# Moving a grouped-query attention into the middle of a differential attention, and turning its value product round

## The chip, the cores and the metric

The kernel runs on one core of a Trainium2 chip. The metric is the device time of one execution in microseconds (us); the time before is the median of three runs. A profile is one execution recorded by the hardware profiler. PE is TensorE's matmul unit and PEld its weight loads, DVE is VectorE, ACT is ScalarE, POOL is GpSimd, SP is the engine that issues most of the transfers.

## The reference, cut to what matters

One transformer layer is computed for 512 latent tokens and 128 context tokens of width 1024, all in fp32. A token mixer with three groups of heads reads one modulated input; its outputs are concatenated and projected, and a squared-ReLU MLP follows.

```python
# group A: 4 heads, two softmax maps per head, values 128 wide
s = einsum('bqhmd,bkhmd->bhmqk', qb, k) * HEAD_DIM ** -0.5
p = softmax(s); w = p[:, :, 0] - lam * p[:, :, 1]
oa = einsum('bhqk,bkhe->bqhe', w, v)            # then RMS norm per head and token
# group B: a gated linear recurrence (scan) over chunks of 64 tokens
# group C: 4 query heads on 2 key/value heads, 64 wide
s = einsum('bqngd,bknd->bngqk', qb, k) * HEAD_DIM ** -0.5
oc = einsum('bngqk,bknd->bqngd', softmax(s), v)
mixed = concatenate([oa, ob, oc], -1) @ w_out
x = layernorm(ALPHA * x + g1 * mixed); hid = square(relu(mod(x) @ w_ff1))
y = layernorm(ALPHA * x + g2 * (hid @ w_ff2))
```

A latent token attends to 512 latent keys and 256 cached context keys, 768 in all. Context tokens attend to the 128 context keys alone.

## The kernel before

The 640 tokens are five tiles of 128 (`NT`): tile 0 is the context, tiles 1 to 4 are latent. Projections take the modulated input `xh`, `xl` (a value split by `split`, L89, into a high and a low part) against weights split in the same way, as three matmuls for each of eight blocks of the width (`mm3`, L126). Ahead of attention stand group B's scans and the projections of A's head 0; behind it stand the output projection (tiles `pswo`), the two MLP products (`psf`, `psy`) and the norms.

In the attention part a "unit" is one head of A and one latent tile t (`a_unit`, L805; 16 units, named A01 to A34 by head and t), or one query head j of C and one tile (`c_unit`, L932; 16 units, named C10 to C43 by t and j). Each unit has three steps:

- s1: the score product into a PSUM tile `pss` of 768 columns, the row maximum `nm` on DVE, and the exponential with its sum on ACT (`softmax_map`, L700). A unit of A has two maps, which DVE joins into one (L814). A unit of C has one, and DVE multiplies it by the reciprocal of its sum (L939).
- transposition of the 128x768 map in six pieces by PE (tiles `pst`, L720), copied to SBUF half by ACT and half by DVE (tiles `pT`).
- s3: the product with the values (`psav`). For A (`av`, L728) the transposed map is the stationary operand, the tokens come out on the partitions, and DVE scales the result (L821). ACT then squares it, and after a head's last tile `a_norm` (L764) normalizes the head, transposes it back (tiles `psao`) and writes `mixed`. For C (L952) the values, 64 wide, are the stationary operand and the transposed map moves through. Two query heads with the same values go to the two halves of the partitions, so that C's output stands already transposed; ACT copies it to `mixed` (L954).

`pipeline` (L828) emits step n's s1, then the transposition of unit n-1, then s3 of unit n-2, and whatever a table (`put`, from L1100 on) hangs behind step n: tiles of the next head's projection, its preparation (`prep`: transposing queries and keys and splitting them, L657 and L671; `prep_ctx`: the head's context tokens), pieces of the modulation (`ada`) and the rest of group B. The framework's scheduler then fixes one order of instructions on each engine; an engine works through its own order and waits wherever it must. PSUM has two buffers for each of three kinds of tile (`ps_mm`, `ps_o`, `ps_s`, L284 to L290); `pss` takes `ps_s`, the projections and C's transposed queries and keys take `ps_mm`.

The order of heads is A0, A1, A2, A3, C. Projections of the next head stand among the units of the one before; C, the last, has none to stand among its own. Once `mixed` is complete for a block of the width, `split` makes the output projection's input from it, for tokens 0 to 383 and then for 384 to 639.

Of the kernel before, what the change touches and what calls it, by code (L numbers as in the profile page):

```python
# [19 lines left out]
P = 128  # L20
# [43 lines left out]
def hybrid_layer_kernel(ctx: ExitStack, tc: tile.TileContext, T):  # L64
# [563 lines left out]
    def new_grp(name, par, ck, cv):  # L628
        g = Grp()
        g.name = name  # L630
        g.par = par
        g.qtags = ("a_q0", "a_q1", "b_b1", "b_k1") if name == "C" else ("a_q0", "a_q1", "b_k0", "b_k1")
        g.ltags = ("a_kl", "u6", "u3", "b_b0")
        g.src = (ck, cv)
        g.z = []
        return g
# [98 lines left out]
    def a_gemm(h):  # L735
        g = new_grp(f"A{h}", h % 2, T["cache_a_k"][:, h * P : (h + 1) * P], T["cache_a_v"][:, h * P : (h + 1) * P])
# [68 lines left out]
    def a_unit(g, h, t):  # L805
# [12 lines left out]
        def s3(pT):  # L818
# [4 lines left out]
            if t == NT - 1:  # L823
                a_norm(g, h)
# [20 lines left out]
    def c_gemm():  # L845
        g = new_grp("C", 0, T["cache_c_k"], T["cache_c_v"])
# [39 lines left out]
    def c_ctx(g):  # L886
# [8 lines left out]
        pr = p1t("b_xs", [P, 512], name="cpC")  # L895
# [32 lines left out]
    def c_prep(g):  # L928
        queries(g, [(0, ((0, 0), (1, 0)))])
# [167 lines left out]
    def put(n, *fs):  # L1097
        post.setdefault(n, []).extend(fs)
# [310 lines left out]
```

## Time and profile before

| | |
|---|---|
| median of three runs | 951.87 us (950.09 to 952.92) |
| the profiled execution, its time and its span | 952.96 us, 951.2 us |
| PE busy | 912.9 us (96% of the span), 6133 instructions |
| DVE busy | 573.6 us (60%), 1123 instructions |
| ACT busy | 432.7 us (45%), 916 instructions |
| PE's share of the chain that ended last | 80%; DVE 11%, ACT 3%, DMA 3% |
| mean granted clock of TensorE | 0.986 |

PE is busy nearly throughout, so the stages that matter are those in which it is not, or in which its clock is low. Of the 40 slices on the page the one from 357 to 381 us is marked 8 for PE and 8 for the clock; it lies between A's last projections and C's units. A busy PE is a pipelined one: the record of a matmul includes its passage through the array, so short waits of PE are hidden in its busy time, and what a matmul costs in a row of them is the distance between starts.

### The profile page before, as it was taken

Reading aid. Unit: us, or ns where it says so; the run is one execution under the profiler, and the core shown is the slowest. Engines: PE = TensorE matmul, PEld = TensorE weight load, DVE = VectorE, ACT = ScalarE, POOL = GpSimd, SP = SyncE. Lnnn points to the kernel's source line nnn. Section 1 sums busy time; section 2 is a strip of 40 time slices with the busy share of each in tenths; the row PEclk is TensorE's granted clock in tenths of the full one; section 3 lists DMA queues with packets and bytes.
Section 4 is the critical chain, followed back from the end, with each engine's and each line's share of the span. In section 5 each row is a group of like instructions: output and inputs, shape, how many; then the busy total and the mean of one; then the engine's idle time right before and its main releaser. Section 6 shows DMA issues by size and latency. Waiting matters only on the chain.

```text
span 951.2 us, 15540 instructions
## 1 busy us (share of the span) xinstructions
PE 912.9 (96%) x6133; PEld 792.2 (83%) x6133; DVE 573.6 (60%) x1123; ACT 432.7 (45%) x916; POOL 53.5 (6%) x108
## 2 busy tenths in 40 slices
PE   6989898999999998999999999999999999999996
PEld 4778886889889786678899999999998888888884
DVE  2378998988876888873794313243236343563448
ACT  3566675466664657651583212222225333243320
POOL 2200010210100000001000000000000000000000
PEclk9998999999999998999999999999999999999998
DMA  9951525433021320113223234342122222142102
GB/s 260 290 157 54 157 86 162 108 92 94 19 78 39 117 65 13 68 45 133 89 68 111 61 95 133 121 125 73 61 90 84 72 68 88 34 152 80 67 23 88
DMA packets 95752, 90.82 MB, mean 95 GB/s; under 512 B 5792, under 2 KB 81280, under 8 KB 95680
## 3 DMA queue, kind: packets, MB, share of 16 engines
q1 hardware_dynamic: 91936, 82.50, 28.9%
q0 software_dynamic: 3552, 7.27, 2.5%
q8 instruction: 48, 0.79, 0.3%
q14 instruction: 24, 0.20, 0.1%
q10 hardware_dynamic: 192, 0.08, 0.0%
HBM read 86.41 MB, written 3.41 MB: 94 GB/s over the span
## 4 chain that ended last, share of the span: by engine, by line
PE 80%; DVE 11%; ACT 3%; DMA 3%; issue 1%; SPq 1%; DVEq 0%; ACTq 0%
PE psf L1271 8%; PE psy L130 8%; PE psf L1272 8%; PE psf L1273 8%; PE psy L129 8%; PE psy L128 8%; PE psA L129 2%; PE psA L130 2%; PE psavA L730 2%; PE psA L128 2%; PE pswo L130 2%; PE pswo L129 2%; PE pswo L128 2%; DVE b_st L560 2%; PE psavC L952 2%
## 5 line engine op out<-in xcount | busy, mean ns | idle before, releaser
L1271 PE MATMUL psf<-xh,wf_h 128*128 128x320 f32 x512 | 158.7, 310 | 0.0
L1272 PE MATMUL psf<-xl,wf_h 128*128 128x320 f32 x512 | 158.1, 309 | 0.0
L1273 PE MATMUL psf<-xh,wf_l 128*128 128x320 f32 x512 | 158.1, 309 | 0.0
L130 PE MATMUL psy<-wg_h,xl 128*128 128x512 f32 x320 | 127.7, 399 | 0.0
L129 PE MATMUL psy<-wg_l,xh 128*128 128x512 f32 x320 | 126.1, 394 | 0.0
L128 PE MATMUL psy<-wg_h,xh 128*128 128x512 f32 x320 | 125.5, 392 | 0.0
L91 DVE TENSOR_TENSOR xl<-hid,xh 128x640 fp32r<-128x640 f32 x64 | 52.1, 824 | 86.5 <-ACT xh L90 86.5
L90 ACT CAST xh<-hid 128x640 fp32r<-128x640 f32 x64 | 45.6, 727 | 121.7 <-PE psy L129 116.2
L1271 PEld LDWEIGHTS psf<-xh,wf_h 128*128 128x128 f32 x512 | 96.3, 188 | 1.7 <-issue 1.2
L1272 PEld LDWEIGHTS psf<-xl,wf_h 128*128 128x128 f32 x512 | 96.3, 188 | 0.0
L1273 PEld LDWEIGHTS psf<-xh,wf_l 128*128 128x128 f32 x512 | 96.3, 188 | 0.0
L1276 DVE TENSOR_TENSOR hid<-hid,psf 128x320 f32<-128x320 f32 x64 | 31.1, 486 | 106.5 <-ACT hid L1275 106.4
L1275 ACT ACTIVATE hid<-psf 128x320 f32<-128x320 f32 x64 | 28.0, 438 | 119.9 <-PE psf L1273 119.9
L129 PEld LDWEIGHTS psy<-wg_l,xh 128*128 128x128 f32 x320 | 60.1, 188 | 15.6
L128 PEld LDWEIGHTS psy<-wg_h,xh 128*128 128x128 f32 x320 | 60.1, 188 | 14.3
L130 PEld LDWEIGHTS psy<-wg_h,xl 128*128 128x128 f32 x320 | 60.1, 188 | 13.7
L91 DVE TENSOR_TENSOR wf_l<-wf_r,wf_h 128x1024 fp32r<-128x1024 f32 x32 | 39.2, 1224 | 37.5 <-ACT wf_h L90 37.5
L128 PE MATMUL psA<-wa_h,xh 128*128 128x384 f32 x160 | 55.2, 346 | 0.0
L130 PE MATMUL psA<-wa_h,xl 128*128 128x384 f32 x160 | 54.9, 344 | 0.0
L129 PE MATMUL psA<-wa_l,xh 128*128 128x384 f32 x160 | 54.7, 343 | 0.0
L90 ACT CAST wf_h<-wf_r 128x1024 fp32r<-128x1024 f32 x32 | 33.7, 1054 | 32.8 <-PE psf L1272 28.4
L91 DVE TENSOR_TENSOR wg_l<-wg_r,wg_h 128x1024 fp32r<-128x1024 f32 x32 | 39.2, 1224 | 7.1 <-ACT wg_h L90 4.5
(475 smaller groups left out, 1897.2 us busy)
## 6 DMA issues: line engine op xcount, KB each, us to landing
wad<-in_w_ada SPq DMA_DIRECT2D x32, 512.0 KB, 4.8
wf_r<-in_w_ff SPq DMA_DIRECT2D x32, 512.0 KB, 3.9
wg_r<-in_w_ff SPq DMA_DIRECT2D x32, 512.0 KB, 3.6
adaw<-in_w_ada SPq DMA_DIRECT2D x32, 256.0 KB, 5.4
wa_r<-in_w_in SPq DMA_DIRECT2D x48, 128.0 KB, 2.9
wo_r<-in_w_out SPq DMA_DIRECT2D x8, 512.0 KB, 3.7
x<-in_x_sample SPq DMA_DIRECT2D x8, 256.0 KB, 4.9
wc_r<-in_w_in SPq DMA_DIRECT2D x4, 512.0 KB, 3.7
```

Of the source, the lines that this page charges most:

```text
L90: A.copy(hi, src)
L91: V.tensor_tensor(lo, src, f32(hi), op=ALU.subtract)
L128: PE.matmul(ps, s[0], m[0], start=start, stop=False)
L129: PE.matmul(ps, s[0], m[1], start=False, stop=False)
L130: PE.matmul(ps, s[1], m[0], start=False, stop=stop)
L560: V.scalar_tensor_tensor(dst, st[r, c, :], dec[r, c : c + 1], u(r, c), op0=ALU.mult, op1=ALU.add)
L730: PE.matmul(po, pT[:, c, :], vals(g, c, c0, n), start=(c == 0), stop=(c == NKC - 1))
L1271: PE.matmul(ps[:, 0:HALF], h, xh[:, k, sl], start=(k == 0), stop=False)
L1272: PE.matmul(ps[:, 0:HALF], h, xl[:, k, sl], start=False, stop=False)
L1273: PE.matmul(ps[:, 0:HALF], l, xh[:, k, sl], start=False, stop=(k == NK - 1))
L1275: A.activation(hs, ps[:, 0:HALF], AF.Relu)
L1276: V.tensor_tensor(hs, hs, ps[:, 0:HALF], op=ALU.mult)
```

## The change

C moves from behind A3 to between A0 and A1, and its sixteen units are ordered by value head n first and tile t second. The table of what stands behind which unit is new: C's projection stands among A0's units, A1's among C's, A2's behind C's last units and among A1's, A3's among A2's, and A3 comes last. C's buffers change with its neighbours. In `c_unit` the map is no longer scaled. The transposed map becomes the stationary operand, as in A; the values, 64 wide, move; DVE scales the 128x64 output by the reciprocal (in place of L939); and when a value head is complete, four transpositions and one copy put it into `mixed`. For the last head `a_norm` runs twice, for tiles 0 to 2 and for tiles 3 and 4.

```diff
-        g.qtags = ("a_q0", "a_q1", "b_b1", "b_k1") if name == "C" else ("a_q0", "a_q1", "b_k0", "b_k1")
-        g.ltags = ("a_kl", "u6", "u3", "b_b0")
+        qt, lt = ("a_q0", "a_q1", "b_k0", "b_k1"), ("a_kl", "u6", "u3", "b_b0")
+        g.qtags, g.ltags = (qt[2:] + qt[:2], lt[2:] + lt[:2]) if name == "C" else (qt, lt)
...
-        tags = ("u4", "u5", "a_vh", "a_vl") if name[0] == "C" else ("u4", "u5")
-        pT = p1t(tags[next(pt_count) % len(tags)], [P, NKC, P], name=f"pT{name}")
+        pT = p1t(("u4", "u5")[next(pt_count) % 2], [P, NKC, P], name=f"pT{name}")
...
-    def a_norm(g, h):
-        A.activation(g.ss, g.ss, AF.Ln, scale=1.0 / P, bias=epsA)
-        A.activation(g.ss, g.ss, AF.Exp, scale=-0.5)
-        for lo, hi in ((0, 1), (1, NT)):
+    def a_norm(g, h, *spans):
+        ss = g.ss[:, spans[0][0] : spans[-1][1]]
+        A.activation(ss, ss, AF.Ln, scale=1.0 / P, bias=epsA)
+        A.activation(ss, ss, AF.Exp, scale=-0.5)
+        for lo, hi in spans:
...
-            if t == NT - 1:
-                a_norm(g, h)
+            if h < NHA - 1:
+                if t == NT - 1:
+                    a_norm(g, h, (0, 1), (1, NT))
+            elif t in (2, NT - 1):
+                a_norm(g, h, (0, 3) if t == 2 else (3, NT))
...
     def c_unit(g, t, j):
         nm = f"C{t}{j}"
+        n = j // 2
 
         def s1():
-            sm = p1t("c_sm", [P, 1], bufs=3, name=f"sm{nm}")
-            pr = softmax_map(g, j, t, sm, 0, nm)
-            V.reciprocal(sm, sm)
-            V.tensor_scalar(pr, pr, sm, None, op0=ALU.mult)
+            rs = p1t("a_rs", [P, 3], bufs=4, name=f"rs{nm}")
+            pr = softmax_map(g, j, t, rs, 0, nm)
+            V.reciprocal(rs[:, 1:2], rs[:, 0:1])
+            g.rs[t, j] = rs
             return pr
 
         def s3(pT):
-            if j % 2 == 0:
-                g.pT = pT
-                return
-            if j == 1:
-                g.po = ps_mm(f"psavC{t}")
-            n = j // 2
-            for c in range(NKC):
-                v = vals(g, c, n * HD, HD)
-                for r, w in ((slice(0, HD), g.pT), (slice(HD, P), pT)):
-                    PE.matmul(g.po[r, n * P : (n + 1) * P], v, w[:, c, :], start=(c == 0), stop=(c == NKC - 1))
-            if j == 3:
-                A.copy(mixed[:, 6:8, t * P : (t + 1) * P], g.po[:, 0:256].rearrange("p (i n) -> p i n", i=2))
+            if t == 1 and j % 2 == 0:
+                g.o = p1t(("ao2", "ao")[n], [P, NLAT // P, P], name=f"co{n}")
+            po = ps_o(f"psav{nm}")
+            av(po[:, 0:HD], g, pT, n * HD, HD)
+            V.tensor_scalar(g.o[:, t - 1, j % 2 * HD : (j % 2 + 1) * HD], po[:, 0:HD], g.rs[t, j][:, 1:2], None, op0=ALU.mult)
+            if t == NT - 1 and j % 2:
+                pt = ps_o(f"psco{n}")
+                for i in range(NLAT // P):
+                    PE.transpose(pt[:, i * P : (i + 1) * P], g.o[:, i, :], ident)
+                A.copy(mixed[:, 6 + n, P:NTOK], pt)
...
+    order = [("a", 0, t, 0) for t in range(1, NT)]
+    order += [("c", NHA, t, 2 * n + j) for n in range(2) for t in range(1, NT) for j in range(2)]
+    order += [("a", h, t, 0) for h in range(1, NHA) for t in range(1, NT)]
...
-    put(13, lambda: tiles(4, 0))
+    put(3, lambda: prep_ctx(4))
+    put(26, lambda: tiles(3, 3, 4))
```

**C's preparation, PE.** From here on a row is one instruction of an engine's order: line, operation, output tile<-operands, shape. Names carry a running number. Before, from the last of C's transposed queries (`psqC0`) and keys (`pskC0`) on, through the transposition of the cached keys (`pskC512`):

```order
L678 MATMUL psqC0_4336<-ident_62,zC4_4279 128x128
L665 MATMUL pskC0_4355<-ident_62,zC4_4279 128x128
L720 MATMUL pstA330_4395<-ident_62,pA330_4297 128x128 x3
L720 MATMUL pstA331_4400<-ident_62,pA330_4297 128x128 x3
L730 MATMUL psavA32_4405<-zA31_3649,pTA32_4312 128x128
L730 MATMUL psavA32_4405<-zA32_3739,pTA32_4312 128x128
L730 MATMUL psavA32_4405<-zA33_3769,pTA32_4312 128x128
L730 MATMUL psavA32_4405<-zA34_3843,pTA32_4312 128x128
L730 MATMUL psavA32_4405<-ckvA3_3848,pTA32_4312 128x128 x2
L705 MATMUL pssC10_4416<-k0C_4353,qC0_4341 128x512
L706 MATMUL pssC10_4416<-k0C_4353,qlC0_4342 128x512
L665 MATMUL pskC512_4364<-ident_62,ckvC_4333 128x128 x2
```

After, from the same two instructions on, through C's context scores (`psccs`) to the first projection matmul of A1:

```order
L678 MATMUL psqC0_3029<-ident_62,zC4_2984 128x128
L665 MATMUL pskC0_3048<-ident_62,zC4_2984 128x128
L665 MATMUL pskC512_3057<-ident_62,ckvC_3026 128x128 x2
L922 MATMUL pscC_3110<-ident_62,zC0_2718 128x128 x3
L894 MATMUL psccs_3119<-cqkC_3108 128x128 x2
L894 MATMUL psccs_3119<-cqkC_3108,cqC_3109 128x128 x2
L128 MATMUL psA10_3146<-wa1_h0_2996,xh_69 128x384
```

Before, the transpositions of unit A33, the product of A32 and C10's first scores stood between C's last transposed tile and `pskC512`. Now `pskC512`, C's transposed context (`pscC`) and its scores follow directly, and A1's projection comes behind them.

**C's preparation, ACT.** After, the row of ACT from the first copy of C's transposed queries to the copies of its transposed context, which `psccs` reads (four more copies like the last one follow):

```order
L686 ACTIVATE qC0_3034<-psqC0_3029 64x512
L668 CAST k0C_3046<-pskC0_3048 64x512
L710 ACTIVATE pA040_3072,smA04_3064<-pssA040_3065,nmA040_3070 128x768
L710 ACTIVATE pA041_3081,smA04_3064<-pssA041_3074,nmA041_3079 128x768
L688 ACTIVATE qC0_3034<-psqC0_3029 64x512
L686 ACTIVATE qC1_3040<-psqC0_3029 64x512
L668 CAST k1C_3047<-pskC0_3048 64x512
L761 ACTIVATE sqA02_3106,ass0_2586<-ao0_2585 128x128
L90 CAST wa2_h0_3702<-wa2_r0_3700 128x768
L688 ACTIVATE qC1_3040<-psqC0_3029 64x512
L668 CAST k0C_3046<-pskC512_3057 64x256
L923 COPY cqkC_3108<-pscC_3110 128x128
```

Before, the unit of A among these copies was A33 and C's first exponentials; now it is A04, with a weight split for A2 (`wa2_h0`).

**The end of the attention part, PE.** Before, from C's last transposition to the first matmul of the output projection:

```order
L720 MATMUL pstC431_5009<-ident_62,pC43_4975 128x128 x3
L952 MATMUL psavC4_4990<-pTC43_5003,zC1_4156 64x128
L952 MATMUL psavC4_4990<-pTC42_4979,zC2_4197 64x128
```

(eight more of L952 follow, two for each block of keys, and then)

```order
L952 MATMUL psavC4_4990<-pTC43_5003,ckvC_4333 64x128
L1181 MATMUL psabg100_5088<-grows_64,sel_63 128x512
L1181 MATMUL psabg101_5092<-grows_64,sel_63 128x512
L128 MATMUL pswo00_5119<-wo0_h0_5097,xh_69 128x512
```

After, from the last head's first norm (`psao30`) on:

```order
L771 MATMUL psao30_5004<-ident_62,ao3_4699 128x128
L719 MATMUL pstA340_5013<-ident_62,pA340_4966 128x128
L771 MATMUL psao30_5004<-ident_62,ao3_4699 128x128
L719 MATMUL pstA340_5013<-ident_62,pA340_4966 128x128
L719 MATMUL pstA341_5018<-ident_62,pA340_4966 128x128 x3
L729 MATMUL psavA33_5023<-zA31_4522,pTA33_4981 128x128
```

(the rest of that product and the six matmuls of unit A34's follow, and then)

```order
L729 MATMUL psavA34_5033<-ckvA3_4661,pTA34_5012 128x128 x2
L771 MATMUL psao33_5045<-ident_62,ao3_4699 128x128 x2
L1179 MATMUL psabg100_5112<-grows_64,sel_63 128x512
L1179 MATMUL psabg101_5116<-grows_64,sel_63 128x512
L128 MATMUL pswo00_5143<-wo0_h0_5121,xh_69 128x512
```

The output projection stood behind a unit of C; now it stands behind A3's last unit and behind the transposition of its norm (`psao33`).

**The end of the attention part, DVE.** After, a piece of DVE's row ahead of the output projection:

```order
L708 TENSOR_REDUCE nmA331_4929<-pssA331_4924 128x1
L91 TENSOR_TENSOR wo1_l0_5302<-wo1_r0_5301,wo1_h0_5303 128x1024
L722 COPY pTA32_4937<-pstA321_4943 128x384
L708 TENSOR_REDUCE nmA340_4964<-pssA340_4959 128x1
L812 RECIPROCAL rsA33_4933<-smA33_4914 128x2
L821 TENSOR_SCALAR ao3_4699<-psavA31_4948,rsA31_4791,lam_647 128x128
L813 SCALAR_TENSOR_TENSOR rsA33_4933<-smA33_4914,lam_647,rsA33_4933 128x1
L708 TENSOR_REDUCE nmA341_4973<-pssA341_4968 128x1
L814 SCALAR_TENSOR_TENSOR pA330_4922<-pA331_4931,rsA33_4933,pA330_4922 128x768
L91 TENSOR_TENSOR xl_70<-mixed_83,xh_69 128x384
L91 TENSOR_TENSOR xl_70<-mixed_83,xh_69 128x256
L722 COPY pTA33_4981<-pstA331_4987 128x384
```

Before, these steps of A3 stood among the evacuations of C's projection, and C's units followed. Now the row holds the last units of A and splits for the output projection (`wo`, `xl`), with no projection of another head beside it.

## Rows read from the trace of the kernel before

**Rows 1.** The page, busy us, share of the span and instructions of engines.
```profile
PE 912.9 (96%) x6133; PEld 792.2 (83%) x6133; DVE 573.6 (60%) x1123; ACT 432.7 (45%) x916; POOL 53.5 (6%) x108
```
**Rows 2.** Windows: length; busy of PE, PEld, DVE, ACT, POOL; clock, DMA share, GB/s.
```profile
199.00:353.00 154.00, 152.48 (x950) 134.45 (x950) 124.97 (x251) 93.52 (x235) 13.25 (x22) 1.00 0.24 73
359.00:384.00 25.00, 20.41 (x125) 16.27 (x124) 21.59 (x42) 18.66 (x53) 0.52 (x1) 0.86 0.06 22
384.00:426.00 42.00, 40.56 (x349) 29.39 (x348) 33.24 (x64) 24.96 (x54) 3.22 (x6) 1.00 0.14 45
```
**Rows 3.** Timeline, C's preparation: start, length, engine, instruction, [idle <-releaser].
```profile
360.03 0.33 PE L678 MATMUL psqC<-ident,zC 128*128 128x128 f32 x1 [1.00 <-DVE zC L623]
...
365.31 0.59 ACT L688 ACTIVATE qC<-psqC 64x512 fp32r<-64x512 f32 x1
...
365.90 0.38 PE L665 MATMUL pskC<-ident,ckvC 128*128 128x128 f32 x2
```
**Rows 4.** Timeline, PE's value products, A's then C's, and maps of C.
```profile
252.27 1.16 PE L730 MATMUL psavA<-zA,pTA 128*128 128x128 f32 x8
253.26 0.61 PE L730 MATMUL psavA<-ckvA,pTA 128*128 128x128 f32 x4
253.63 0.36 PE L706 MATMUL pssA<-k0A,qlA 128*128 128x256 f32 x1
...
397.80 0.98 PE L952 MATMUL psavC<-pTC,zC 128*64 128x128 f32 x13 [0.29 <-ACT pTC L725]
...
399.25 0.50 PE L705 MATMUL pssC<-k0C,qC 128*128 128x512 f32 x1
...
400.85 0.84 PE L720 MATMUL pstC<-ident,pC 128*128 128x128 f32 x6
```
**Rows 5.** Timeline, weight loads ahead of matmuls with 2 and 64 columns.
```profile
186.95 0.52 PEld L976 LDWEIGHTS psada<-selc,ada 128*128 128x128 f32 x4
187.49 0.75 PEld L553 LDWEIGHTS psu<-mixed,b_kht 64*128 64x128 f32 x12
```
**Rows 6.** Groups of ACT, 199:426: count | busy us, mean ns | idle before.
```profile
L710 ACT ACTIVATE pA<-pssA,nmA 128x768 f32<-128x768 f32 x32 | 28.8, 902 | 3.3 <-DVE nmA L708 2.9 <-PE pstA L720 0.3
L90 ACT CAST wa_h<-wa_r 128x768 fp32r<-128x768 f32 x9 | 7.5, 830 | 3.8 <-PE psA L130 3.6 <-DMA wa_r<-in_w_in 0.2
L686 ACT ACTIVATE qA<-psqA 64x512 fp32r<-64x512 f32 x7 | 4.1, 590 | 0.6 <-PE psqA L678 0.4
L923 ACT ACTIVATE cqkC<-pscC 64x128 f32<-64x128 f32 x1 | 0.3, 274 | 0.0
```
**Rows 7.** Groups of DVE, 199:426, same columns.
```profile
L708 DVE TENSOR_REDUCE nmA<-pssA 128x1 f32<-128x768 f32 x32 | 30.2, 952 | 2.3 <-PE pssA L706 1.9
L814 DVE SCALAR_TENSOR_TENSOR pA<-pA,rsA,pA 128x768 f32<-128x768 f32 x16 | 16.2, 1013 | 0.2
L939 DVE TENSOR_SCALAR pC<-pC,smC 128x768 f32<-128x768 f32 x16 | 9.8, 613 | 0.0
L723 DVE COPY pTA<-pstA 128x384 f32<-128x384 f32 x16 | 8.8, 552 | 2.5 <-PE pstA L720 2.5
L821 DVE TENSOR_SCALAR ao<-psavA,rsA,lam 128x128 f32<-128x128 f32 x16 | 6.5, 407 | 5.5 <-PE psavA L730 5.5
L91 DVE TENSOR_TENSOR wo_l<-wo_r,wo_h 128x1024 fp32r<-128x1024 f32 x5 | 6.0, 1207 | 0.0
L687 DVE SCALAR_TENSOR_TENSOR qlA<-psqA,qA 64x512 fp32r<-64x512 f32 x7 | 4.8, 687 | 0.7 <-ACT qA L686 0.5
L91 DVE TENSOR_TENSOR xl<-mixed,xh 128x256 fp32r<-128x256 f32 x6 | 2.5, 416 | 0.3 <-ACT xh L90 0.3
```
**Rows 8.** Timeline of DVE, first and last of 24 instructions nearly without a gap.
```profile
349.65 0.55 DVE L868 TENSOR_TENSOR zn<-psC,css 128x384 f32<-128x384 f32 x1
...
361.10 0.68 DVE L687 SCALAR_TENSOR_TENSOR qlC<-psqC,qC 64x512 fp32r<-64x512 f32 x1 [0.19 <-ACT qC L686]
```
**Rows 9.** Timeline of PE: the first matmul of the output projection.
```profile
426.15 0.40 PE L128 MATMUL pswo<-wo_h,xh 128*128 128x512 f32 x1
```

More of the change, by code (lines that the diff above doesn't have):

```diff
@@ L845, in c_gemm @@
     def c_gemm():
-        g = new_grp("C", 0, T["cache_c_k"], T["cache_c_v"])
+        g = new_grp("C", 1, T["cache_c_k"], T["cache_c_v"])
         g.kcol = 256
@@ L928, in c_prep @@
     def c_prep(g):
+        g.rs = {}
         queries(g, [(0, ((0, 0), (1, 0)))])
@@ L1089, in hybrid_layer_kernel, with make @@
     prep_ctx(0)
-    nu = NT - 1
-    units = [None] * (NHA * nu + 4 * nu)
+    order = [("a", 0, t, 0) for t in range(1, NT)]
+    order += [("c", NHA, t, 2 * n + j) for n in range(2) for t in range(1, NT) for j in range(2)]
+    order += [("a", h, t, 0) for h in range(1, NHA) for t in range(1, NT)]
+    units = [None] * len(order)
     pre, post = {}, {}
-    for h in range(NHA):
-        for t in range(1, NT):
-            n = h * nu + t - 1
-            pre.setdefault(n, []).append(lambda n=n, h=h, t=t: units.__setitem__(n, a_unit(gr[h], h, t)))
+    def make(n, kind, h, t, j):
+        units[n] = a_unit(gr[h], h, t) if kind == "a" else c_unit(gr[h], t, j)
+    for n, u in enumerate(order):
+        pre.setdefault(n, []).append(lambda n=n, u=u: make(n, *u))
     def put(n, *fs):
@@ L1100, in hybrid_layer_kernel @@
     put(0, lambda: b_out(3, parts[3]))
-    put(0, lambda: start(1))
-    put(0, lambda: tiles(1, 0))
-    put(1, lambda: tiles(1, 1))
-    put(1, lambda: tiles(1, 2))
-    put(1, lambda: tiles(1, 3))
-    put(1, lambda: tiles(1, 4))
-    put(2, lambda: b_final())
-    put(2, lambda: start(2))
-    put(2, lambda: prep(1))
-    put(2, lambda: prep_ctx(1))
-    put(3, lambda: tiles(2, 0))
-    put(4, lambda: tiles(2, 1))
-    put(6, lambda: tiles(2, 2))
-    put(6, lambda: tiles(2, 3))
-    put(6, lambda: tiles(2, 4))
@@ L1116, in hybrid_layer_kernel @@
-    put(6, lambda: prep(2))
-    put(6, lambda: prep_ctx(2))
-    put(7, lambda: ada(1, "b_b1"))
-    put(8, lambda: start(3))
-    put(8, lambda: tiles(3, 0))
-    put(8, lambda: tiles(3, 1))
-    put(9, lambda: tiles(3, 2))
-    put(9, lambda: tiles(3, 3))
-    put(10, lambda: tiles(3, 4))
-    put(10, lambda: prep(3))
-    put(10, lambda: prep_ctx(3))
-    put(13, lambda: start(4))
-    put(13, lambda: tiles(4, 0))
-    put(13, lambda: tiles(4, 1))
-    put(13, lambda: tiles(4, 2))
-    put(13, lambda: tiles(4, 3))
@@ L1132, in hybrid_layer_kernel @@
-    put(13, lambda: tiles(4, 4))
-    put(14, lambda: prep(4))
-    put(16, lambda: queries(gr[NHA], [(P, ((2, 1), (3, 1)))]))
-    put(18, lambda: prep_ctx(4))
-    put(19, lambda: ada(11, "b_k0"))
-    put(20, lambda: ada(8, "b_k0"))
-    for t in range(1, NT):
-        for j in range(4):
-            n = NHA * nu + (t - 1) * 4 + j
-            pre.setdefault(n, []).append(lambda n=n, t=t, j=j: units.__setitem__(n, c_unit(gr[NHA], t, j)))
+    put(0, lambda: start(4))
+    put(0, lambda: tiles(4, 0, 1))
@@ new lines, in hybrid_layer_kernel @@
+    put(1, lambda: tiles(4, 2, 3))
+    put(2, lambda: b_final())
+    put(2, lambda: tiles(4, 4))
+    put(2, lambda: start(1))
+    put(2, lambda: prep(4))
+    put(3, lambda: prep_ctx(4))
+    put(3, lambda: tiles(1, 0))
+    put(6, lambda: tiles(1, 1))
+    put(9, lambda: tiles(1, 2))
+    put(9, lambda: queries(gr[NHA], [(P, ((2, 1), (3, 1)))]))
+    put(11, lambda: tiles(1, 3))
+    put(13, lambda: tiles(1, 4))
+    put(15, lambda: start(2))
+    put(16, lambda: prep(1))
+    put(17, lambda: prep_ctx(1))
@@ L1142, in hybrid_layer_kernel @@
+    put(18, lambda: tiles(2, 0))
+    put(19, lambda: ada(1, "b_b1"))
+    put(21, lambda: tiles(2, 1, 2))
+    put(22, lambda: tiles(2, 3, 4))
+    put(22, lambda: start(3))
+    put(22, lambda: prep(2))
+    put(23, lambda: prep_ctx(2))
+    put(24, lambda: tiles(3, 0))
+    put(25, lambda: tiles(3, 1, 2))
+    put(26, lambda: tiles(3, 3, 4))
+    put(26, lambda: prep(3))
+    put(27, lambda: prep_ctx(3))
+    put(28, lambda: ada(11, "b_b1"))
+    put(29, lambda: ada(8, "b_b1"))
     pipeline(units, pre, post)
```

4 lines of the change are left out of this document (2 added, 2 removed).

## The prediction

> **What bounds the kernel now.** I read the page's engine line first: PE is busy 96% of the span [rows 1], so the reader should look for the places where it is not, or is slow. The windows by stage give them. From 199 to 353 us (A's heads with their projections) PE is busy 152.48 of 154 us at full clock; there is nothing to win there by order. From 359 to 384 it is busy 20.41 of 25 at a mean granted clock of 0.86, and from 384 to 426 it is busy 40.56 of 42 [rows 2]. That is the stretch of C, which has no next head's projection to fill with. Visible idle is 4.6 + 1.4 = 6.0 us, and 25 x 0.14 = 3.5 us are lost to the clock: 9.5 us at least.
>
> Some waits hide inside PE's busy time, so I price the work instead. In a dense piece two maps of scores take 399.25 to 400.85, 0.80 each, and six transpositions 0.84 with the passage through the array, some 0.70 without [rows 4]. A product of A takes 252.27 to 253.63 for 12 matmuls, 1.36 us or 113 ns each. C's product shows 22 records from 397.80 to 399.25, 66 ns each; for the twelve that one unit needs, 0.80 us [rows 4]. The 16 units of C are 16 x (0.80 + 0.70 + 0.80) = 36.8 us. What else PE does after 359 (three products of A, two transpositions, some 20 single transpositions, the modulation's pieces, the context's small products) comes to about 14 us by the same distances. The output projection begins at 426.15 [rows 9], 67.2 us after 359: 67.2 - 50.8 = 16 us are lost around C.
>
> **The change, part by part.**
>
> *C's lost time goes, at its old place: -16 us* (bounds -9.5, the visible part alone, and -18, if the distances above hold waits too). Its new place has A1's projection. But of 16 units only some have a projection tile behind them, and a map, an exponential and a copy still follow one another; for those without I keep 1.5 us, a tenth.
>
> *C's product, turned round.* The moving side shrinks to 64 columns, and 128x128 maps become the stationary side. No row shows this shape. Next to it lie A's product, the same load with 128 columns (113 ns), and four loads of 128x128 whose matmuls move 2 columns, in 0.52 us, at most 130 ns each [rows 5]. If 2 columns cost about as much as 128, it is the load that sets the distance, and 64 will too: 1.36 us for a unit, 0.56 more than before, times 16 = **+9.0 us**. The other row in the neighbourhood is that of twelve loads of 64 rows in 0.75 us, 63 ns [rows 5]; they are half as tall and lie in two halves of the array, as C's old operands did with their 64 columns, so I hold it to be the farther one. By it the term is 0. If the old product really ran at 60 ns, 24 in 1.45 us, the term is 16 x 0.64 = 10. Bounds 0 and +10. The Trainium skill, "TensorEngine Tiling (Array Packing)", section "When to Use Tiling", speaks against this edit: for a right side of at most 64 columns it advises swapping the operands and tiling the columns, for up to twice the rate, which is what the kernel before does. By that the new product would cost twice the old, 16 x 0.80 = 12.8 us more instead of 9; the two rows agree in direction, with 113 against 66.
>
> *Transpositions of C's output*: eight at 0.11 (the 0.70 above over six) = **+0.9 us** on PE.
>
> *The map's scaling on DVE*, 16 x 613 ns = 9.8 us [rows 7], goes; 16 scalings of 128x64 come, each at most the 407 ns of 128x128 [rows 7], 6.5 us. DVE has idle time among C's units (33.24 busy of 42 [rows 2]), so I take nothing for it; if DVE were the bound there, it would be a gain of 3.3 us. The two copies that take the place of four ACT copies, the buffers' new names and `a_norm` in two pieces issue no DMA; SP's and POOL's orders hold the same transfers with C's and A1's weights exchanged, at a DMA share of 0.24 [rows 2], at nothing. If a weight came late there, the price would be a matmul's wait, at most the 3.6 us by which ACT waited for PE in its weight casts over 227 us [rows 6].
>
> *C's preparation at its new place: +10 us* (6 to 14). PE's order is now: C's last transposed queries and keys, the cached keys (`pskC512`), the context (`pscC`), its scores (`psccs`), and only then A1's first projection. An engine waits in its order, so a wait ahead of `psccs` holds the filler back too. The first wait is for `zC4`. Before, PE waited 1.00 us for it [rows 3]; now two splits of A1's weights stand in front on DVE, 128x768 each, estimated at 768/1024 of 1207 ns [rows 7], 0.9 us, and group B's last two passes, against a split of `wo`, two maxima and a copy before: some 1.4 us more, so 2.4. The second wait is for ACT. `pskC512` needs the buffer that `psqC0` leaves when its last copy ends: before, 365.31 + 0.59 = 365.90, the moment it started, 5.5 us after `psqC0` ended [rows 3]. PE had A33's transposition, A32's product and C10's scores to do meanwhile, and now has nothing. ACT's row up to `psccs` is seven copies of queries and keys at 590 ns, two exponentials of A04 at 902, the new cast of `wa2` at 830 and five copies of the context at 274 [rows 6]: 4.1 + 1.8 + 0.8 + 1.4 = 8.1 us, of which PE covers 0.5 with its own transpositions. 2.4 + 7.6 = 10. It is 6 if ACT has done two exponentials and both keys early; 14 if the clock falls after the idle time as it did before (3.5 us in 25 [rows 2]). This is most of what C lost at its old place, and it moves along.
>
> *The end of attention: +15 us* (11 to 21). A3's last units now have no projection beside them, and the output projection's splits have come in their place. Between A24's scores and `pswo` DVE has some 75 instructions [rows 7]: 10 maxima at 952, 5 combinations at 1013, 6 copies of transposed maps at 552, 7 scalings at 407, 4 splits of `wo` at 1207, 6 of `xl` at about 416, 2 of queries at 687, and some 35 small ones that I put at 10 us: 9.5 + 5.1 + 3.3 + 2.8 + 4.8 + 2.5 + 1.4 + 10 = 39.4 us. Records overlap: in a dense row 24 instructions take from 349.65 to 361.10 [rows 8], where their lengths sum to 13.05, 0.07 less each; so 39.4 - 5 = 34.5 us. Behind DVE's last combination (A34's) follow its transposition, two copies, the product, scaling, square, norm, `psao33` and the copies into `mixed`, one after another: 0.7 + 0.55 + 2.7 (two products) + 0.4 + some 3 = 7.5. PE's path is then 42 us long. PE's own work in it is 10 maps, 6 transpositions, 7 products and small pieces: 8.0 + 4.2 + 9.5 + 5 = 27. So 15 us of idle that no other work fills: `pswo` stands behind `psao33`. Bounds: 11 if the norm's chain lies beside the splits, 21 if the clock is at half for 12 us of it.
>
> *Sum*: 9.0 + 0.9 - 16 + 1.5 + 10 + 15 = +20.4 us. The profiled execution is 952.96 us with a span of 951.2, 1.1 us above the median; from the median, 951.87 + 20.4 = **972 us**, and `pswo` starts near 426 + 20 = 446.
>
> **The rivals.**
>
> *The gaps fill (other side).* C's loss goes and at the two new places the scheduler's order leaves PE work enough: ACT ends C's copies while PE is still in A0's product, DVE keeps pace with A3. Then the sum is 9.9 - 14.5 = -4.6: 947 us. It decides where the two new waits together cost less than 4.6 us. For it: in A's stage DVE is busy 125 of 154 us [rows 2] and does not stop PE. Against it: there the projections are the cover, and the order shows none at either place.
>
> *The product is priced by its moving columns.* Then 64 columns take half of 113 ns, 0.68 us a unit, 0.12 less than before, and the term is -1.9 in place of 9: 20.4 - 10.9 = +9.5, 961 us. For it: the 63 ns row [rows 5]. Against: the 2-column loads. [...]
>
> *Both new places at their upper bounds*: 14 and 21 in place of 10 and 15, +30.4, 982 us; in its favour the clock at half after idle time in C's old place.
>
> *Nothing moves*: gain and losses cancel, or C's waits merely change place at the same size: 952.
>
> **How the numbers follow.** Forecast 972: 0.57. Gaps fill, 947: 0.14. Product by columns, 961: 0.12. Upper bounds, 982: 0.12. Nothing, 952: 0.05. The range leaves out the first rival and a little of the upper one: 951 to 983. A measurement of this kernel can tell about 0.3% (2.9 us) from no change. Faster by more: 0.14, and 0.02 from the low tail of the product's case with the other terms at their low ends, 0.16; within: 0.05; slower: 0.79.
>
> **What would show it.** Right: product records of C 110 to 113 ns apart, not 66; C's units without visible idle; PE waiting some 2 us for `zC4` and 7 to 8 us on ACT ahead of `pskC512` and `psccs`; in the last 42 us ahead of `pswo` PE busy only about 27, DVE over 85%; `pswo` near 446, and from there on the same 525 us as before. Wrong: records at 57 to 66 ns (9 us too many); PE over 90% busy ahead of `pswo` (15 too many); A1's projection among C's preparation instead of behind it (10 too many).

## The result, and the profile after

The changed kernel takes 982.0 us (980.88 to 983.10), the kernel before beside it on the same chip 952.39; the ratio is 1.0313 with a 95% interval of 1.029 to 1.0335. That is 3.1% slower, some 29.6 us, inside the range of the prediction and 10 us above its 972. The profiled execution has a span of 979.7 us, 28.5 more than before.

The engine line of the page after answers to [rows 1]. PE works 11.7 us more, and its share falls from 96% to 94%:

```profile
PE 924.6 (94%) x6141; PEld 809.8 (83%) x6141; DVE 569.6 (58%) x1123; ACT 434.7 (44%) x916; POOL 53.5 (5%) x108
```

The windows by stage answer to [rows 2]; the columns are the same: stretch, length, busy us of PE, PEld, DVE, ACT and POOL with their instructions, granted clock, DMA share, GB/s.

```profile
240.00:250.00 10.00, 2.13 (x11) 1.24 (x9) 9.11 (x16) 6.97 (x14) 1.03 (x2) 0.73 0.44 119
250.00:265.00 15.00, 14.35 (x76) 12.79 (x77) 5.50 (x12) 6.39 (x23) 1.07 (x2) 0.72 0.12 37
...
280.00:330.00 50.00, 49.70 (x347) 44.97 (x347) 31.02 (x67) 26.08 (x57) 2.08 (x4) 1.00 0.15 45
...
407.00:453.30 46.30, 32.41 (x207) 26.38 (x208) 35.31 (x74) 28.39 (x75) 3.22 (x6) 0.88 0.21 68
```

C's units (280 to 330) now run beside A1's projection without idle time and at full clock. The loss at C's old place is gone, and two new ones have come: from 240 to 250 PE is busy 2.13 of 10 us, with a low clock behind it until 265, and in the 46.3 us ahead of the output projection it is busy 32.41, at a clock of 0.88. The output projection begins at 453.31, as the timeline further down shows; before it was 426.15 [rows 9], so 27.2 of the 28.5 us are lost by then. The other 1.3 lie in its first matmuls, 0.63 us each in place of 0.40, since the clock is still at the lower level when they begin.

The timeline of PE shows C's product, in answer to [rows 4]: twelve matmuls of 128x64 between 279.97 and 281.33 (columns: start, length, engine, instruction).

```profile
279.97 1.11 PE L729 MATMUL psavC<-zC,pTC 128*128 128x64 f32 x8
280.91 0.61 PE L729 MATMUL psavC<-ckvC,pTC 128*128 128x64 f32 x4
281.33 0.48 PE L706 MATMUL pssC<-k0C,qlC 128*128 128x512 f32 x1
```

That is 1.36 us or 113 ns each, the same as A's product with 128 moving columns [rows 4]. Half the columns cost the same.

C's preparation, in answer to [rows 3], is shown by the timeline of all engines; the idle time of the engine ahead of an instruction and what ended it stand in brackets:

```profile
242.79 0.33 PE L678 MATMUL psqC<-ident,zC 128*128 128x128 f32 x1 [1.75 <-DVE zC L623]
...
248.45 0.69 DVE L669 TENSOR_TENSOR k1C<-pskC,k1C 64x512 fp32r<-64x512 f32 x1
...
249.25 0.66 PE L665 MATMUL pskC<-ident,ckvC 128*128 128x128 f32 x2 [6.02 <-issue]
...
249.47 0.59 ACT L688 ACTIVATE qC<-psqC 64x512 fp32r<-64x512 f32 x1
...
250.12 0.90 PE L922 MATMUL pscC<-ident,zC 128*128 128x128 f32 x3 [0.21 <-ACT qC L688]
...
251.54 0.79 PE L894 MATMUL psccs<-cqkC 64*128 64x128 f32 x2 [0.52 <-ACT cqkC L925]
```

PE waits 1.75 us for the last tile of C's projection (the page's name for it is `zC`), then 6.02 for the cached keys' transposition, and 0.73 more ahead of the context's scores: 8.5 us. The page names no releaser for the long one; it ends 0.11 us after DVE's last reading of the transposed keys (248.45 + 0.69 = 249.14), and the next, `pscC`, 0.06 after ACT's last copy of the transposed queries (249.47 + 0.59). By these times both wait for a PSUM buffer of the ring that C's queries, keys and all projections share; the run with the other ring, below, tests it.

The end of the attention part, timeline of PE:

```profile
438.14 0.85 PE L719 MATMUL pstA<-ident,pA 128*128 128x128 f32 x6 [2.07 <-DVE pA L814]
439.23 2.08 PE L729 MATMUL psavA<-zA,pTA 128*128 128x128 f32 x8 [0.24 <-ACT pTA L724]
441.10 1.06 PE L729 MATMUL psavA<-ckvA,pTA 128*128 128x128 f32 x4
444.08 0.30 PE L771 MATMUL psao<-ident,ao 128*128 128x128 f32 x1 [1.92 <-DVE ao L770]
...
445.87 1.96 PE L729 MATMUL psavA<-zA,pTA 128*128 128x128 f32 x8
447.63 1.06 PE L729 MATMUL psavA<-ckvA,pTA 128*128 128x128 f32 x4
...
452.26 0.53 PE L771 MATMUL psao<-ident,ao 128*128 128x128 f32 x2 [1.83 <-DVE ao L770]
452.54 0.97 PE L1179 MATMUL psabg<-grows,sel 128*128 128x512 f32 x2
453.31 0.63 PE L128 MATMUL pswo<-wo_h,xh 128*128 128x512 f32 x1
```

The units of A wait for DVE's combination (2.07 us at A33's), the norms' transpositions `psao` wait for their scalings (1.92 and 1.83), and behind two of these waits a product runs at the lower clock: its first eight matmuls take 1.87 us (439.23 to 441.10) and 1.76 (445.87 to 447.63) in place of 0.99 [rows 4].

DVE ends its last combination, A34's, at 440.56 + 1.02 = 441.58 (timeline of DVE). The windows from A24's scores, the last ahead of A3's own, up to that moment, and from there to the output projection:

```profile
440.56 1.02 DVE L814 SCALAR_TENSOR_TENSOR pA<-pA,rsA,pA 128x768 f32<-128x768 f32 x1
```

```profile
404.79:441.58 36.79, 26.88 (x182) 21.39 (x181) 34.10 (x68) 25.73 (x64) 2.67 (x5) 0.92 0.27 85
441.58:453.31 11.73, 7.42 (x41) 6.45 (x40) 3.42 (x10) 4.04 (x14) 0.55 (x1) 0.79 0.07 22
```

DVE is busy 34.10 of the first 36.79 us, 93%, and 3.42 of the 11.73 behind them, in which one step waits for the one before.

### The profile page after: what moved, and what is told of

Same layout as the page of the kernel before. It is cut to its first block, busy times and chain, and to the rows that moved or that the text cites. A ratio compares the mean times of both kernels' runs of the same rounds, so it can differ in the third digit from the quotient of the medians.

```text
span 979.7 us, 15551 instructions
## 1 busy us (share of the span) xinstructions
PE 924.6 (94%) x6141; PEld 809.8 (83%) x6141; DVE 569.6 (58%) x1123; ACT 434.7 (44%) x916; POOL 53.5 (5%) x108
## 4 chain that ended last, share of the span: by engine, by line
PE 79%; DVE 8%; DMA 5%; ACT 4%; SPq 2%; issue 1%; POOL 0%; DVEq 0%; ACTq 0%; POOLq 0%
PE psf L1269 8%; PE psy L130 8%; PE psf L1271 8%; PE psf L1270 8%; PE psy L129 8%; PE psy L128 8%; PE psavA L729 3%; PE psavC L729 2%; PE psA L130 2%; PE psA L129 2%; PE psA L128 2%; PE pswo L128 2%; PE pswo L129 2%; PE pswo L130 2%; DMA adaw<-in_w_ada 1%
## 5 line engine op out<-in xcount | busy, mean ns | idle before, releaser
L130 PEld LDWEIGHTS psy<-wg_h,xl 128*128 128x128 f32 x320 | 60.1, 188 | 13.9
```

What stands on the lines that cost most here:

```text
L130: PE.matmul(ps, s[1], m[0], start=False, stop=stop)
```

## The experiments

Times of different groups of runs are compared by their ratio to the kernel before beside them; a difference of two ratios is known to about 0.3%, 3 us.

### The old product for half of C's units

```diff
-        pT = p1t(("u4", "u5")[next(pt_count) % 2], [P, NKC, P], name=f"pT{name}")
+        tags = ("u4", "u5", "a_kd0", "a_kd1") if name[0] == "C" and name[2] in "01" else ("u4", "u5")
+        pT = p1t(tags[next(pt_count) % len(tags)], [P, NKC, P], name=f"pT{name}")
...
+        if n == 0:
+            return s1_old, s3_old, nm
```

`s1_old` and `s3_old`, cut here, are the steps of the kernel before: a scaled map, the values stationary, two heads in the two halves.

> The changed kernel with the product turned back for the eight units of C's first value head alone: scaled maps, the values 64 wide as the stationary operand, two query heads in the two halves, as in the kernel before. The load theory (128x128 stationary maps cost 1.36 us a unit where the old product costs 0.80) gives 8 x 0.56 + 0.45 for four transpositions = 5 us less than the changed kernel: about 977 us. If the product's price lies hidden under ACT or DVE in that dense stretch, or the old product has no advantage there, it stays at 982; if the scaling of the map on DVE (eight times 0.61 us) binds, it is above 982.

974.96 us, ratio 1.0242 (1.0215 to 1.0268): 0.7% or 6.8 us below the changed kernel. The timeline of PE shows a pair of units in the old form, this time with all 24 of its matmuls recorded:

```profile
276.16 1.09 PE L956 MATMUL psavC<-pTC,zC 128*64 128x128 f32 x16
277.09 0.61 PE L956 MATMUL psavC<-pTC,ckvC 128*64 128x128 f32 x8
277.62 0.50 PE L706 MATMUL pssC<-k0C,qlC 128*128 128x512 f32 x1
```

24 matmuls from 276.16 to 277.62 are 61 ns each, 0.73 us a unit. The turn costs 1.36 - 0.73 = 0.63 us a unit, so eight units 5.0 and four transpositions 0.45. The measured 6.8 agrees within its uncertainty. The scalings that came back on DVE cost nothing that shows.

### The turned product alone, in the kernel before

```diff
-            pr = softmax_map(g, j, t, sm, 0, nm)
...
-            V.tensor_scalar(pr, pr, sm, None, op0=ALU.mult)
...
+            pr = softmax_map(g, j, t, rs, 0, nm)
...
-                    PE.matmul(g.po[r, n * P : (n + 1) * P], v, w[:, c, :], start=(c == 0), stop=(c == NKC - 1))
...
+            av(po[:, 0:HD], g, pT, n * HD, HD)
+            V.tensor_scalar(g.co[n][:, t - 1, j % 2 * HD : (j % 2 + 1) * HD], po[:, 0:HD], g.rs[t, j][:, 1:2], None, op0=ALU.mult)
```

> The kernel before, order and all, with the product of C alone turned round and the factor at its output. The load theory gives 9.0 for the product, 0.9 for eight transpositions and about 1.5 for a last chain of product, scaling, transposition and copy ahead of the output projection: 952 + 11 = 963 us. If the waits that lie inside C's old stretch (16 us) absorb the dearer product, or the map's scaling on DVE was what PE waited for, it comes out at 952 to 956.

961.2 us, ratio 1.0095 (1.0076 to 1.0115): 9.2 us slower than the kernel before, order and places unchanged. So about a third of the change's loss comes from the product, and C's waits did not absorb it. It is a little under the 11 expected; by the 0.63 of the run before, the product and the transpositions would be 11.0, which is at the upper end of what the ratio's interval allows (0.0115 x 952 = 10.9).

### C's context put later, behind A1's first tile

```diff
-    put(3, lambda: prep_ctx(4))
     put(3, lambda: tiles(1, 0))
+    put(5, lambda: prep_ctx(4))
```

> The changed kernel with C's context scores put two steps later and A1's first projection tile ahead of them; PSUM buffers as they are. If PE's idle time in C's preparation comes from C's transposed cached keys, which wait for a PSUM buffer of the same ring as the projections, that wait of 6 us stays and only the later ones go: 1 to 3 us less, 979 to 981 us. If it comes from the context's scores that hold the filler back, nearly all of it goes: 970 us.

980.53 us, ratio 1.0296 (1.0276 to 1.0316), 1.6 us less. The timeline of PE shows which waits stay:

```profile
247.59 0.80 PE L705 MATMUL pssC<-k0C,qC 128*128 128x512 f32 x1 [3.81 <-DVE rsA L813]
249.71 0.66 PE L665 MATMUL pskC<-ident,ckvC 128*128 128x128 f32 x2 [0.90 <-issue]
250.58 0.69 PE L128 MATMUL psA<-wa_h,xh 128*128 128x384 f32 x1 [0.21 <-ACT qC L688]
```

A1's projection starts at 250.58, directly behind the cached keys, where it stood behind the context's scores; but waits of 3.81 and 0.90 stay ahead of it, where the changed kernel has one of 6.02. The context's scores were the smaller part. By the releaser that the timeline names, ACT's last copy of the transposed queries, the projection could not have come earlier, whatever the table says: its PSUM buffer is one that C's queries hold.

### C's queries and keys in the other PSUM ring

```diff
-            pk = (ps_mm if g.name == "C" else ps_o)(f"psk{g.name}{lo}")
+            pk = ps_o(f"psk{g.name}{lo}")
...
-            pq = (ps_mm if g.name == "C" else ps_o)(f"psq{g.name}{col}")
+            pq = ps_o(f"psq{g.name}{col}")
```

> The changed kernel with C's transposed queries and keys in the PSUM ring of the transposed maps (as A's are) in place of the ring of the projections; the table is as it was. The theory of the missing cover: A1's projection can now fill in ahead of and between C's queries and keys, PE's idle 8.5 us there and some 4 us of low clock behind it go, 10 to 12 us less: 970 to 972 us. The rival, that ACT's and DVE's chain sets the time whatever stands beside it, because C's first scores need their results: at most 3 us less, 979 us or more.

970.93 us, ratio 1.0189 (1.0162 to 1.0216), 11.8 us less than the changed kernel, with the table as it was. The windows of the same place:

```profile
242.00:252.00 10.00, 9.35 (x57) 8.22 (x55) 8.92 (x14) 7.89 (x21) 0.98 (x2) 1.00 0.49 137
252.00:265.00 13.00, 13.00 (x97) 11.32 (x96) 10.02 (x22) 8.60 (x26) 2.27 (x4) 1.00 0.08 25
```

PE is busy 9.35 of the 10 us from 242 to 252 and the clock stays up. ACT and DVE are about as busy as in the changed kernel (7.89 and 8.92 us here, 6.97 and 9.11 there): they did not become faster, PE had only been kept from the work that lay beside. This is nearly the whole of the loss at C's new place.

### Weight splits of the output projection on POOL

```diff
-        wk = wslots(f"wo{n}", T["w_out"], ((n * 512, 512),), 2)
+        wk = wslots(f"wo{n}", T["w_out"], ((n * 512, 512),), 2, eng=G if n == 0 else None)
```

> The changed kernel with the subtraction in the first four weight splits of the output projection (128x1024) on POOL in place of DVE. If DVE's queue sets the time of the last stretch (35 us busy of the 47 ahead of the output projection), four instructions of 1.21 us less on it bring up to 4.6 us: 977.5 to 979. If the stretch is a chain of ACT, PE and DVE steps, each waiting for the one before, the splits lie in its gaps: 981 to 982. If POOL is so slow with them that the output projection waits for its weights, above 982.

988.73 us, ratio 1.0369 (1.0344 to 1.0393): 5.3 us above the changed kernel. The timeline of POOL and DVE shows why this run says nothing of a DVE with less to do:

```profile
404.28 4.86 POOL L91 TENSOR_TENSOR wo_l<-wo_r,wo_h 128x1024 fp32r<-128x1024 f32 x2 [16.79 <-ACT wo_h L90]
...
404.48 2.47 DVE L91 TENSOR_TENSOR xl<-mixed,xh 128x256 fp32r<-128x256 f32 x1 [0.83 <-ACT xh L90]
406.87 0.41 DVE L617 TENSOR_TENSOR zA<-psA,rope_c 128x256 f32<-128x256 f32 x1
...
407.53 1.90 DVE L91 TENSOR_TENSOR xl<-mixed,xh 128x256 fp32r<-128x256 f32 x1
```

DVE's subtraction for `xl`, 0.42 us otherwise [rows 7], takes 2.47 and 1.90 beside POOL's two, which together end at 404.28 + 4.86 = 409.14, and the second ends at 409.43, just behind them; the one between, which reads PSUM, keeps its 0.41. DVE was not relieved but held up.

### The last head's norm undivided

```diff
-            if h < NHA - 1:
-                if t == NT - 1:
-                    a_norm(g, h, (0, 1), (1, NT))
-            elif t in (2, NT - 1):
-                a_norm(g, h, (0, 3) if t == 2 else (3, NT))
+            if t == NT - 1:
+                a_norm(g, h, (0, 1), (1, NT))
```

> The changed kernel with the last head's norm undivided, behind its last tile, as in the kernel before. The theory: 3 scalings, 3 transpositions and a copy of 0.6 us move from beside A33 into the last chain, where nothing covers them: 1 to 2.5 us more, 983 to 984.5. If the first half of the norm, which stood in PE's order ahead of A34's transposition (a wait of 1.9 us at 444), cost as much as it saved, it is 981 to 982.

977.4 us, ratio 1.0253 (1.0234 to 1.0272): 5.7 us less, where I expected a little more or nothing. The timeline of PE, in answer to the end shown above:

```profile
440.07 1.16 PE L729 MATMUL psavA<-zA,pTA 128*128 128x128 f32 x8 [0.24 <-ACT pTA L724]
441.06 0.61 PE L729 MATMUL psavA<-ckvA,pTA 128*128 128x128 f32 x4
442.56 0.84 PE L719 MATMUL pstA<-ident,pA 128*128 128x128 f32 x6 [0.89 <-DVE pA L814]
443.70 1.16 PE L729 MATMUL psavA<-zA,pTA 128*128 128x128 f32 x8 [0.30 <-ACT pTA L724]
...
448.54 1.11 PE L771 MATMUL psao<-ident,ao 128*128 128x128 f32 x5 [1.89 <-DVE ao L770]
...
449.95 0.40 PE L128 MATMUL pswo<-wo_h,xh 128*128 128x512 f32 x1
```

```profile
441.40 1.02 DVE L814 SCALAR_TENSOR_TENSOR pA<-pA,rsA,pA 128x768 f32<-128x768 f32 x1
```

```profile
404.99:449.95 44.96, 32.58 (x220) 25.99 (x219) 37.02 (x77) 28.55 (x75) 3.22 (x6) 0.92 0.23 76
```

In the changed kernel A34's transposition stood in PE's row behind the first half of the norm: DVE had ended A34's combination at 441.58, and PE its work on A32's product some 0.6 us later, but PE waited for the norm's scaling until 444.08. Undivided, the transposition starts as soon as the combination is done (441.40 + 1.02 = 442.42), eight matmuls of a product take records of 1.16 us in place of 1.96 to 2.08, and the output projection begins at 449.95 and at once with matmuls of 0.40. From the end of the combination to the output projection are 7.53 us in place of 11.73. 3.4 us are gained by its start and about 1.3 behind it; the whole norm at the end costs no more than its second half did, since both wait the same 1.9 us.

A part of this is the clock and not the norm: A32's product stands ahead of either form of the norm, behind the same wait of 2.07 us, and its first eight matmuls take 0.99 us here (440.07 to 441.06) and 1.87 in the changed kernel. The other profiles bound the norm's part. In the changed kernel and the six other runs that keep the divided norm and A3's single products (the old product for half of C, the later context, the other ring, the splits on POOL, A1's products twice, the low part left out), the piece behind the combination takes 10.3 to 11.8 us; with the norm undivided it takes 7.5 here and 8.0 in the run with three parts undone. So the divided norm costs 2.3 to 4.3 us there.

### Extra work for PE at the end, and in a place without idle time

```diff
-            av(po[:, 0:P], g, pT, 0, P)
+            for _ in range(2 if h == 3 else 1):        # in the control: h == 1
+                av(po[:, 0:P], g, pT, 0, P)
```

> The changed kernel with A3's four value products each made twice: 4 x 1.36 = 5.4 us of work more for PE in the last stretch. If PE has nothing to do there for some 14 us, three of the four disappear in the idle time and only A34's, which lies on the last chain, costs 1.4 (2 at half clock): 983 to 984.5. A busier PE may also hold its clock and give a little back. If that idle time can't be used (PE is late whenever it is wanted), it costs the full amount: 987.

> The control to A3's doubled product: the same 5.4 us of PE work more, in A1's four units, where PE shows no idle time. Both theories expect the full amount there: 987 us. If it is less, PE has hidden slack among A's units with projections too, and the doubled product says nothing about the last stretch.

With A3's products twice: 984.47 us beside 953.91, ratio 1.0307 (1.0269 to 1.0344), the same as the changed kernel's 1.0313. With A1's: 989.04 us, ratio 1.0368 (1.0352 to 1.0383), 5.2 us more. So 5.4 us of work cost their full price where PE is dense, and in the last stretch nothing that the times show; but the interval of the first is wide, 3.6 us to either side. Its profile is sharper. The windows of the run with A3's products twice, cut as above at the end of A34's combination:

```profile
406.54:443.68 37.14, 29.69 (x205) 24.27 (x204) 34.06 (x68) 25.77 (x64) 2.67 (x5) 0.91 0.25 85
443.68:457.48 13.80, 9.49 (x66) 8.68 (x65) 3.42 (x10) 4.05 (x14) 0.55 (x1) 0.86 0.06 19
```

Ahead of the combination PE is busy 2.8 us more than in the changed kernel (29.69 and 26.88) in a stretch that is 0.35 longer (37.14 and 36.79): that work lies in time that PE had free. Behind it PE is busy 2.07 more and the stretch is 2.07 longer: what A33's and A34's products cost there, on the last chain, is paid in full.

### DVE relieved in another way

```diff
-                split(hi, lo, raw)
+                if nolow:
+                    A.copy(hi, raw)
+                    lv = hv
+                else:
+                    split(hi, lo, raw)
...
-        wk = wslots(f"wo{n}", T["w_out"], ((n * 512, 512),), 2)
+        wk = wslots(f"wo{n}", T["w_out"], ((n * 512, 512),), 2, nolow=n == 0)
```

This kernel leaves out the low part of half of `w_out`; the high part stands in its place in the matmuls.

> The changed kernel without the low half of the first four weight splits of the output projection: the high half stands in its place in the matmuls, so as many matmuls run, and DVE has four instructions of 1.21 us less ahead of the output projection (left out: the low part of half of w_out). The earlier try to move them to POOL slowed DVE's own instructions (0.42 us ones took 1.9 to 2.5 beside POOL's), so it did not tell. If DVE's queue sets the last stretch's time, up to 4.6 us less: 977 to 979.5. If the chain of each unit (maximum, exponential, combination, transposition, product) sets it and the splits lie in its gaps: 981 to 982.

982.56 us, ratio 1.031 (1.0286 to 1.0334): no change, though DVE has 5 us less to do. The windows:

```profile
407.00:453.00 46.00, 32.29 (x188) 27.60 (x186) 29.93 (x66) 25.34 (x68) 3.23 (x6) 0.81 0.15 48
```

DVE is busy 29.9 us in place of 35.3, and the output projection still begins at 453.88. So a shorter row of DVE alone did not shorten the stretch. That DVE's row did not set its length in the changed kernel is not shown by it: PE's clock is lower here (0.81 against 0.88, and 0.66 from 410 to 420), which takes up to 46.0 x 0.07 = 3.2 us more, much of the 4.6 that the relief could bring, and the scheduler's order around it is another one.

### Three parts undone at once

```diff
-            pk = (ps_mm if g.name == "C" else ps_o)(f"psk{g.name}{lo}")
+            pk = ps_o(f"psk{g.name}{lo}")
...
-            elif t in (2, NT - 1):
-                a_norm(g, h, (0, 3) if t == 2 else (3, NT))
+            if t == NT - 1:
+                a_norm(g, h, (0, 1), (1, NT))
...
+        if n == 0:
+            return s1_old, s3_old, nm
```

These are lines of the three edits shown above, each made in full.

> The changed kernel with three of its parts undone or mended at once: C's queries and keys in the other PSUM ring (measured alone: 11.8 us less), the last head's norm undivided (5.7 less), the old product for C's first value head (6.8 less). If the three costs lie at three places of PE's row and don't share time, they add: 982 - 24 = 958 us. If they share (a wait that ends early at one place is taken up at the next), it stays above 962. What is then left against the kernel before is the other half of the product (5 us) and the idle time of A3's last units less what C's old place had lost.

961.96 us, ratio 1.01 (1.0073 to 1.0127): 20.3 us below the changed kernel where the three alone sum to 24.3. The four missing are about the uncertainty of that sum, and 961.96 lies between the 958 of costs that add and the 962 above which they were to share time, so the run does not tell which. Two thirds of the loss are thus taken back while C stays in the middle; the kernel before remains 9 us faster.

### C's projection earlier, in the kernel before

```diff
-    put(13, lambda: start(4))
-    put(13, lambda: tiles(4, 0))
...
+    put(12, lambda: start(4))
+    put(12, lambda: tiles(4, 0))
...
-    put(14, lambda: prep(4))
+    put(13, lambda: prep(4))
```

> The kernel before with C's projection begun one unit earlier and its preparation put behind A32 in place of A33, so that two units of A stand beside the wait for its queries and keys, and no other edit. If the time lost around C's old place comes from a preparation without cover, a part of its 16 us goes: 944 to 949. If it is a bound of ACT and DVE there (both are over 75% busy from 359 to 384), it moves and 950 to 954 remains; if A3's units then lack the projection as cover, as in the changed kernel, it is above 954.

> The same, and C's queries and keys in the PSUM ring of the transposed maps. In the changed kernel this ring brought 11.8 us, because a projection could run beside. Here no projection stands beside them but A3's maps and products, which use the ring themselves: I expect no more than 2 us to either side of the run with the earlier projection alone. If the ring itself was what cost, it is 5 us or more below it.

955.54 us, ratio 1.0027 (1.0013 to 1.004), and with the other ring 958.95, ratio 1.0065 (1.0044 to 1.0086). Neither beats the kernel before. In the first, the wait of 1.00 us for the last tile [rows 3] falls to 0.18, and another of 2.54 ahead of C's first scores comes with it:

```profile
362.23 0.33 PE L678 MATMUL psqC<-ident,zC 128*128 128x128 f32 x1 [0.18 <-DVE zC L623]
365.21 0.80 PE L705 MATMUL pssC<-k0C,qC 128*128 128x512 f32 x1 [2.54 <-ACT qC L688]
```

From 359 to 384 PE is busy 20.26 us, as against 20.41 before [rows 2]. The stretch has no projection, wherever the preparation stands in it. The ring, worth 11.8 us where a projection stood beside it, is worth nothing here and costs 3.6 us, where no more than 2 were expected. A3's transpositions and products use it too, but that this is the reason is not shown.

## Why the prediction held, and which terms were off

**The sign and the mechanism held**: three new costs against one gain, in the places named. The size was too small: 20.4 us were added up and 29.6 measured, and the time lies only 1 us below the upper end of the range. Term by term:

- *The product*: forecast 9.0 + 0.9. The records are 113 ns apart as forecast; the old ones were 61 apart, not 66, since two records were missing in the row [rows 4]. That makes 16 x 0.63 = 10.1 + 0.9, the upper bound of 10 that the prediction named; alone the turned product measured 9.2. The choice between the two neighbouring rows [rows 5], the taller load for the nearer one, was right. The rival that prices by moving columns falls.
- *C's preparation*: forecast 10, of it 2.4 for the last tile and 7.6 behind it. Visible are 1.75 and 6.02 + 0.73, and with the low clock behind them 11.8 by the run with the other ring. The step that failed in part is the name of the buffer: by the times, `pskC512` waited for the buffer of the transposed keys, which DVE releases, and `pscC` for that of the queries. The sum came out because both are fed by the same ACT row.
- *The end*: forecast a path of 42 us from A24's scores to `pswo`, 34.5 of it DVE's row up to A34's combination and 7.5 the chain behind it, with 27 of PE's work, so 15 idle. Measured are 48.5 us: 36.8 up to the end of that combination, with DVE busy 34.10, and 11.7 behind it. 48.52 - 26.88 - 7.42 = 14.2 us are idle, close to the 15, and some 5.3 are lost to the clock (48.5 x 0.11), 19.5 in all, near the upper bound of 21 (PE's busy 34.3 us are then some 29 at full clock, forecast 27); the stretch from 407 on gives the same, 13.9 and 46.3 x 0.12 = 5.6. The step that was mis-sized is the chain behind the combination, 11.7 us in place of 7.5. The prediction counted the split norm among the things that cost nothing, but its first half stands in PE's order ahead of A34's transposition. With the norm whole the chain takes 7.53 us, as forecast, the stretch has 44.96 - 32.58 = 12.4 us of idle time and 45.0 x 0.08 = 3.6 lost to the clock, 16 in all, and the time is 5.7 us lower, of which the norm itself is 2.3 to 4.3. The sign "DVE over 85%" came true only up to the combination (93%); over the last 46.3 us it is 76%.
- *The gain at C's old place*: forecast 16 less 1.5. No run measured it alone. By subtraction, 27.2 = 11.0 + 11.8 + 19.5 - 15.1; the windows after show no idle time among C's units, so it agrees, but it also takes up every error of the other terms (with the 9.2 that the product measured alone it is 13.3), and the losses to the clock in it are upper figures, since a stretch's mean clock counts its idle time too.

The sum of the forecast was 20.4, that of the measured terms, with the gain as the remainder, 27.2 by the start of the output projection and 28.5 by the end. Of the difference of 8.1, 4.5 are the end, 1.8 the preparation, 1.1 the product, 1.3 the low clock in the output projection's first matmuls, which no term held, and -0.6 the gain.

**Of the rivals**, the gaps did not fill, and the price of 4.6 us from which that decides was passed by either place alone. The case of both new places at their upper bounds (14 and 21, 982 us) was nearest in time, but of the two places only the end went near its bound, and the product went to its own.

Open is what sets the 36.8 us up to A34's combination. PE's work does not: 2.8 us more of it cost 0.35. DVE's row, which the prediction took for the path, is 93% busy there and has the forecast length, but the run that shortened it does not settle it, since PE's clock and order changed with it. Only three buffers hold maps and a unit of A takes two, so the second exponential of a unit may wait until the unit before is transposed; a fourth was not tried.

## What to carry to other kernels

A stage moved to where it finds cover takes the cover from another place: before moving it, look at what will stand last, and at whether the work that is to fill a gap can start at all, or needs a buffer of the ring that the waiting stage holds. One look at the PSUM ring was worth more here (11.8 us) than the position in the table (1.6). A 128x128 stationary operand for 64 moving columns costs what 128 columns cost; two half-wide stationary tiles side by side were nearly twice as fast. A small step that is put early so that it is out of the way stands in an in-order row, and whatever is behind it waits for its inputs (2.3 to 4.3 us here).

## What the runs showed of the hardware

A POOL instruction can hold up one of DVE: a DVE subtraction with both inputs in SBUF, 0.42 us alone, took 1.90 to 2.47 beside a POOL subtraction of 128x1024 (2.4 us each) and in the second case ended 0.3 us behind it, while a DVE instruction with one input in PSUM kept its 0.41. The Trainium skill, "SBUF — State Buffer", section "Who interferes with whom", states this as a rule, for DVE instructions with two SBUF inputs against POOL instructions that read SBUF; the trace agrees. The granted clock of TensorE has two levels, 2.4 and 1.2 GHz, and the lower came in stretches in which PE waited, for 1.8 to 6 us at a time: the mean granted clock was 0.72 and 0.73 around C's preparation and 0.88 ahead of the output projection, where the first eight matmuls of a product took 1.87 us in place of 0.99. Not every such wait was followed by it: behind the same wait of 2.07 us they took 1.87 in the changed kernel and 0.99 with the norm undivided. It cost at most 5.6 us beside 13.9 of idle time at the end, and at most 15 x 0.28 = 4.2 beside 8.5 behind C's preparation, where the other ring leaves 11.8 - 8.5 = 3.3 for it.
